# Differential attention of a hybrid decoder step: q and k rows loaded two heads ahead, head 0 prepared amid the projections, and VectorE's small factor and the norm's row written in another form

## The chip, the cores and the metric

One core of a Trainium2 chip runs the whole program in one launch. TensorE multiplies matrices into PSUM, VectorE and ScalarE work element by element on SBUF and PSUM, POOL (GpSimd) does element work and issues DMAs of its own, and SP issues most DMAs. The metric is the time of one execution on the device in microseconds (us). The kernel before takes 2875.54 us, the median of 3 runs (2874.0 to 2877.55).

## The reference

One inference step of a two-layer decoder with fp32 weights: 1024 prompt rows and 16 meta rows (T = 1024, NM = 16), and 8 running sequences of one token each. Layer 0 mixes by gated linear attention, layer 1 by differential attention; each is followed by a squared-ReLU MLP. The change lies in layer 1's prompt part:

```python
def diff_core(q, k, v, q_pos, k_pos, lam):
    s = jnp.einsum('bqhmd,bkhmd->bhmqk', q, k).astype(F32) * (DIFF_DH ** -0.5)
    s = jnp.where(mask, s, -jnp.inf)
    p = jax.nn.softmax(s, axis=-1)
    a = p[:, :, 0] - lam * p[:, :, 1]
    return jnp.einsum('bhqk,bkhe->bqhe', a, v.astype(F32))
...
o = rms_norm(o, g_sub) * (1.0 - lam_init)
```

There are 8 heads, each with two maps m of width 64 over the same values of width 128.

## The kernel before

fp32 products are made from pairs: an operand x is split into a rounded high part and a low part (`split`: ScalarE casts, VectorE subtracts), and three matmuls, high x high, high x low and low x high, are added in PSUM (`mm3`, L187 to L189). All instructions are put in order, engine by engine, by a scheduler that goes by a simulated timeline; on the chip each engine runs its list in order and waits on semaphores. So a source edit can move instructions of other lines.

**Projections** (L1050 to L1089). `XH`, `XL` hold the normalised activations, feature by token, as two halves of 512 tokens. Twelve units u of 256 output columns (u 0 to 3 q, 4 to 7 k, 8 to 11 v) are computed in four blocks of 256 rows (`t2_`). `kunit` loads a unit's weights into the buffers `whi` and `wlo` (two of each). A block's result goes to the buffer `qo` (three of them), is rotated by VectorE if it is q or k, and is written by SP to DRAM (L1078): q to `qd`, k and v to the outputs. The running sequences' decode (`paged`: 512 page loads by SP, element work by VectorE, and small matmuls) is spread over these blocks and most of layer 0.

**Attention** (L1092 on). For each head `prep(h)` loads k and q rows into a `wlo` buffer, the meta keys and the v rows into a `whi` buffer, transposes them on TensorE into the PSUM tile `axt` (L1135, L1140, L1145: 17 transposes) and splits them into the half h % 2 of `XH` and `XL`, which the projections no longer need. For heads 1 to 7, nine DMAs on POOL's queue (`move`, L1151 to L1157) then stack the high and low parts of a map's 64 features in 128 partitions, so that two matmuls do the work of three. Head 0 has no moves: its scores are three matmuls over 64 partitions (L1175 to L1177), those of the others two over 128 (L1179, L1180). `prep(h + 1)` is called ahead of head h's first tile.

`tile_` does one block t of 128 queries: score chunks into `mmt` (three PSUM buffers), VectorE's masked negation with running minimum (L1183, into `as`), ScalarE's exponential with its sum (L1185), the factor -lam l0 / l1 (L1187, L1188), the combination of the two maps (L1189), transposes (L1198), copies (L1200) and the product with v (L1203) into `smt`. After four tiles ScalarE copies the outputs to `Y` (L1238) and the sums of squares are taken (L1239, L1240). After every second head `o_norm` makes the norm's factor, with a power on POOL (L1214), and multiplies the outputs (L1215), on POOL for heads 0 to 6. The buffers of the attention's pools (`as` among them) take memory that the projections' pools (`qo` among them) leave.

Of the kernel before, what the change touches and what calls it, by code (L numbers as in the profile page):

```python
# [21 lines left out]
P = 128  # L22
# [89 lines left out]
def hybrid_step(ctx, tc, A, dbg=None, upto=9):  # L112
# [73 lines left out]
    def mm3(ps, ah, al, bh, bl, first, last):  # L186
        TE.matmul(ps, ah, bh, start=first, stop=False)  # L187
        TE.matmul(ps, ah, bl, start=False, stop=False)  # L188
        TE.matmul(ps, al, bh, start=False, stop=last)  # L189
# [860 lines left out]
    for u in range(12):  # L1050
        hi, lo = kunit(wd, u * 256)
        hv, lv = (x.rearrange("p (k n) -> p k n", n=256) for x in (hi, lo))
        for t2_ in range(4):
            ps = mmt()
            for i in range(2):
                t = 2 * t2_ + i
                a = slice(t * P, (t + 1) * P)
                for k in range(NB):
                    mm3(ps[:, i * 256 : (i + 1) * 256], XH[:, k, a], XL[:, k, a], hv[:, k, :], lv[:, k, :], k == 0, k == NB - 1)
            o = qt.tile([P, 2, 256], F32, name="qo")  # L1060
            S.copy(o.rearrange("p i n -> p (i n)"), ps)
            rows = slice(2 * t2_ * P, (2 * t2_ + 2) * P)
            pr = slice(NM + rows.start, NM + rows.stop)
            if u < 8:
                tmp = qt.tile([P, 2, 4, 16], F32, name="qr")
                pv = ps.rearrange("p (i n d) -> p i n d", i=2, d=64)
                ov = o.rearrange("p i (n d) -> p i n d", d=64)
                tb = rtab[:, 2 * t2_ : 2 * t2_ + 2]
                V.tensor_tensor(ov[:, :, :, 0:16], pv[:, :, :, 0:16], bc(tb[:, :, 0:16], [P, 2, 4, 16], 2), op=ALU.mult)
                V.tensor_tensor(tmp[:, :, :, 0:8], pv[:, :, :, 8:16], bc(tb[:, :, 16:24], [P, 2, 4, 8], 2), op=ALU.mult)  # L1070
                V.tensor_tensor(tmp[:, :, :, 8:16], pv[:, :, :, 0:8], bc(tb[:, :, 24:32], [P, 2, 4, 8], 2), op=ALU.mult)
                steps_v.append(V.tensor_tensor(ov[:, :, :, 0:16], ov[:, :, :, 0:16], tmp, op=ALU.add).ins)
            if u < 4:
                dst = qd[rows, u * 256 : (u + 1) * 256]
            else:
                hs = slice(2 * (u % 4), 2 * (u % 4) + 2)
                dst = A["k_rows_p" if u < 8 else "v_rows_p"][0, 0, pr, hs, :].rearrange("t h d -> t (h d)")
            dma(dst.rearrange("(i p) n -> p i n", p=P), o)  # L1078
            next(paged, None)
        if u == 3:  # L1080
            with tc.issue_after(steps_v[-1]):
                list(alpha_row(A["ln_mlp_g"][0:1], ALU.mult))
        elif u == 6:
# [4 lines left out]
        elif u == 3:  # L1088
            list(paged)  # L1089
# [23 lines left out]
    def prep(h):  # L1113
        kr = A["k_rows_p"][0, 0, :, h, :]
        vr = A["v_rows_p"][0, 0, :, h, :]


        raw = wsp.tile([P, 2048], F32R, name="wlo").bitcast(F32).rearrange("p (i t d) -> p i t d", i=2, d=P)
        kx, qx = raw[:, 0], raw[:, 1]
        vk = wsp.tile([P, 2048], F32R, name="whi").bitcast(F32)  # L1120
        vx = vk[:, :1024].rearrange("p (t d) -> p t d", d=P)
        km, vm = vk[:NM, 1024 : 1024 + P], vms[h % 2]
        dma(kx, kr[NM:].rearrange("(t p) d -> p t d", p=P))
        dma(qx, qd[:, h * P : (h + 1) * P].rearrange("(t p) d -> p t d", p=P))
        dma(km, kr[:NM])
        dma(vm[:NM], vr[:NM])
        dma(vx, vr[NM:].rearrange("(t p) d -> p t d", p=P))
        xh, xl = (x.t[h % 2].rearrange("p a n -> p (a n)") for x in (XH, XL))
        w = NM + T
        k2 = [xh[:, :w], xh[:, w : 2 * w]]  # L1130
        q2 = [xh[:, 2 * w : 2 * w + T], xh[:, 2 * w + T :]]
        kl_, ql2 = xl[:, :w], [xl[:, w : w + T], xl[:, w + T : w + 2 * T]]
        kh_, qh_, ql_ = k2[0], q2[0], ql2[0]
        ps = axt()
        TE.transpose(ps[:, :NM], km, ident[:NM, :NM])  # L1135
        split(kh_[:, :NM], kl_[:, :NM], ps[:, :NM])
        for c in range(2):
            ps = axt()
            for i in range(4):
                TE.transpose(ps[:, i * P : (i + 1) * P], kx[:, 4 * c + i, :], ident)  # L1140
            cs = slice(NM + 512 * c, NM + 512 * c + 512)
            split(kh_[:, cs], kl_[:, cs], ps)
            ps = axt()
            for i in range(4):
                TE.transpose(ps[:, i * P : (i + 1) * P], qx[:, 4 * c + i, :], ident)  # L1145
            cs = slice(512 * c, 512 * c + 512)
            split(qh_[:, cs], ql_[:, cs], ps)
        if h == 0:
            return vm, vx, kh_, qh_, ql_, kl_
        move = nc.gpsimd.dma_start  # L1150
        move(k2[1][64:], kh_[64:])  # L1151
        move(kh_[64:], kl_[:64])
# [415 lines left out]
```

## Time and profile before

| What | us |
|---|---|
| median of 3 runs | 2875.54 |
| the profiled execution | 2875.13 |
| its span | 2873.2 |
| TensorE busy | 2757.3 (96%) |
| VectorE busy | 1974.9 (69%) |
| ScalarE busy | 1083.8 (38%) |
| POOL busy | 1148.1 (40%) |

The span runs from the first to the last instruction. A busy share is an average over stages with different limits, and TensorE's busy time includes the latency of each matmul, so that a busy TensorE is not one at its peak. The views name stretches in us from the span's start; the projections lie at about 1440 to 1775, the attention at 1775 to 2061. In a row of waits stand the waiting engine and line, the releaser, the total, the count and the longest wait.

### The profile page before, as it was taken

The page shows a single profiled execution, that of the slowest core. Times are in us where ns is not written, and L with a number is a line of the kernel's source. Part 1 is how long each engine was busy: PE and PEld are TensorE (multiplying, and loading weights), DVE is VectorE, ACT ScalarE, POOL GpSimd, SP SyncE. Part 2 cuts the span into 40 slices and gives each one's busy share as a digit, 9 for nine tenths or more (in the row PEclk, how much of TensorE's full clock was granted, in tenths as well). Part 3 has the DMA queues.
Part 4 walks back from the last instruction along what each step waited for, and adds up shares of the span by engine and source line. Part 5 has one row for each costly group of instructions (what it writes and reads, how often), then busy time and mean ns, then how long its engine had stood idle before and what let it go on. Part 6 is the DMA issues. An engine that isn't in the chain of part 4 may idle for free. (4 is left out here: it accounts for less than half of the span.)

```text
span 2873.2 us, 52001 instructions
## 1 busy us (share of the span) xinstructions
PE 2757.3 (96%) x19653; PEld 2269.7 (79%) x19653; DVE 1974.9 (69%) x3048; ACT 1083.8 (38%) x2117; POOL 1148.1 (40%) x811
## 2 busy tenths in 40 slices
PE   8889999999999999999999999988999999999997
PEld 5666777997777777777798978878889888797985
DVE  2565544568887778777668711788638888978788
ACT  3233444252221221221331112677525536355553
POOL 1230212334343443433233321032236766777764
PEclk9899999999999999999999998899999999999999
DMA  7557741625798898888569984464334554554573
GB/s 249 180 187 257 250 175 41 245 91 170 282 339 305 319 353 307 322 323 303 198 233 317 363 327 137 89 144 98 118 99 89 114 131 107 136 122 113 128 188 89
DMA packets 276871, 577.28 MB, mean 201 GB/s; under 512 B 24567, under 2 KB 139837, under 8 KB 272525
## 3 DMA queue, kind: packets, MB, share of 16 engines
q1 hardware_dynamic: 252284, 520.66, 51.9%
q0 software_dynamic: 24336, 53.31, 10.7%
q8 instruction: 154, 2.52, 0.4%
q14 instruction: 97, 0.79, 0.1%
HBM read 531.16 MB, written 29.26 MB: 195 GB/s over the span
## 5 line engine op out<-in xcount | busy, mean ns | idle before, releaser
L175 POOL TENSOR_TENSOR wlo<-raw,whi 128x512 fp32r<-128x512 f32 x256 | 372.5, 1469 | 750.5 <-ACT whi L174 669.7
L187 PE MATMUL mmt<-whi,XH 128*128 128x256 f32 (+1 forms) x1760 | 524.5, 300 | 1.1 <-ACT Y L311 0.7
L188 PE MATMUL mmt<-wlo,XH 128*128 128x256 f32 (+1 forms) x1760 | 524.8, 299 | 0.6 <-POOL wlo L175 0.6
L187 PE MATMUL mmt<-XH,whi 128*128 128x512 f32 (+1 forms) x1216 | 436.0, 359 | 7.9 <-DVE HL L184 2.9
L189 PE MATMUL mmt<-whi,XL 128*128 128x256 f32 x1536 | 435.7, 285 | 0.1
L189 PE MATMUL mmt<-XH,wlo 128*128 128x512 f32 (+1 forms) x1216 | 432.2, 356 | 0.0
L174 ACT CAST whi<-raw 128x512 fp32r<-128x512 f32 x256 | 152.6, 619 | 584.1 <-PE mmt L189 181.9
L791 DVE TENSOR_REDUCE sc<-pg 128x16 f32<-128x1024 f32 x256 | 308.3, 1211 | 76.3 <-POOL pg L790 73.8
L188 PEld LDWEIGHTS mmt<-wlo,XH 128*128 128x128 f32 x1760 | 332.1, 189 | 29.0 <-issue 18.1
L187 PEld LDWEIGHTS mmt<-whi,XH 128*128 128x128 f32 x1760 | 331.1, 189 | 25.6 <-issue 11.8
L188 PE MATMUL mmt<-XL,whi 128*128 128x512 f32 x768 | 306.4, 399 | 0.0
L790 DVE TENSOR_TENSOR pg<-pg,qb 128x1024 f32<-128x1024 f32 x192 | 262.3, 1374 | 62.2 <-DMA pg<-in_cache_k 55.4
L189 PEld LDWEIGHTS mmt<-whi,XL 128*128 128x128 f32 x1536 | 289.7, 189 | 11.4 <-issue 10.1
L187 PEld LDWEIGHTS mmt<-XH,whi 128*128 128x128 f32 x1216 | 229.7, 189 | 55.5 <-issue 12.9
L790 POOL TENSOR_TENSOR pg<-pg,qb 128x1024 f32<-128x1024 f32 x64 | 162.3, 2538 | 252.1 <-DMA pg<-in_cache_k 182.6
L189 PEld LDWEIGHTS mmt<-XH,wlo 128*128 128x128 f32 x1216 | 229.8, 189 | 34.5 <-issue 2.1
L187 PE MATMUL mmt<-whi,HH 128*128 128x512 f32 x512 | 204.7, 401 | 4.6 <-DVE Y L1015 4.5
L189 PE MATMUL mmt<-whi,HL 128*128 128x512 f32 x512 | 203.9, 398 | 0.0
L188 PE MATMUL mmt<-wlo,HH 128*128 128x512 f32 x512 | 203.4, 397 | 0.0
L1413 POOL TENSOR_TENSOR wlo<-rw,whi 128x512 fp32r<-128x512 f32 x92 | 157.7, 1779 | 86.2 <-ACT whi L1412 67.7
L1413 POOL TENSOR_TENSOR wlo<-RW,whi 128x512 fp32r<-128x512 f32 x96 | 167.3, 1788 | 53.7 <-ACT whi L1412 53.7
L188 PEld LDWEIGHTS mmt<-XL,whi 128*128 128x128 f32 x768 | 144.9, 189 | 39.1 <-issue 7.9
(440 smaller groups left out, 5837.3 us busy)
## 6 DMA issues: line engine op xcount, KB each, us to landing
pg<-in_cache_k SPq DMA_DIRECT2D x256, 512.0 KB, 6.5
pg<-in_cache_v SPq DMA_DIRECT2D x256, 512.0 KB, 6.4
raw<-in_mlp_w SPq DMA_DIRECT2D x164, 256.0 KB, 4.6
swt<-in_mlp_w SPq DMA_DIRECT2D x32, 1024.0 KB, 5.0
rw<-in_mlp_w SPq DMA_DIRECT2D x116, 256.0 KB, 3.3
RW<-in_mlp_w POOLq DMA_DIRECT2D x96, 256.0 KB, 5.7
raw<-in_gla_w_in SPq DMA_DIRECT2D x48, 256.0 KB, 3.0
swt<-in_gla_w_in SPq DMA_DIRECT2D x12, 1024.0 KB, 4.9
```

Source lines behind the costliest of these rows:

```text
L174: S.copy(hi[:, c], raw)
L175: G.tensor_tensor(lo[:, c], raw, hi[:, c].bitcast(F32), op=ALU.subtract)
L187: TE.matmul(ps, ah, bh, start=first, stop=False)
L188: TE.matmul(ps, ah, bl, start=False, stop=False)
L189: TE.matmul(ps, al, bh, start=False, stop=last)
L790: eng.tensor_tensor(pg, pg, qb, op=ALU.mult)
L791: return V.tensor_reduce(sc[:, n, :], pg.rearrange("p (h d) -> p h d", d=64), op=ALU.add, axis=AX.X).ins
L1413: G.tensor_tensor(lo[:, k, :], t, hi[:, k, :].bitcast(F32), op=ALU.subtract)
```

## The change

q and k rows get buffers of their own (`rqk`, `rkm`, two of each), kept from the projections to the attention's end, and are loaded two heads ahead; the v rows keep their `whi` buffer and are loaded apart. `prep` is cut in two, keys with their three moves first, then queries, and head 0 goes through it as the others do. It is called amid the last blocks of the projections, which are put in an order in which the tokens 0 to 511 are done three blocks before the end. The factor is a scalar_tensor_tensor with one scalar column and a one-column operand. `o_norm` always multiplies on VectorE, in pieces of 512 elements.

```diff
+        return TE.matmul(ps, al, bh, start=False, stop=last)
...
+    rqp = er.enter_context(tc.tile_pool(name="rqp", bufs=2, side="right"))
+    def load_qk(h):
+        raw = rqp.tile([P, 2, 8, P], F32, name="rqk")
+        km = rqp.tile([NM, P], F32, name="rkm")
+        kr = A["k_rows_p"][0, 0, :, h, :]
+        dma(km, kr[:NM])
+        dma(raw[:, 0], kr[NM:].rearrange("(t p) d -> p t d", p=P))
+        dma(raw[:, 1], qd[:, h * P : (h + 1) * P].rearrange("(t p) d -> p t d", p=P))
+        return raw, km
+    def prep(h, raw, km):
...
+        TE.transpose(ps[:, :NM], km, ident[:NM, :NM])
+        split(kh_[:, :NM], kl_[:, :NM], ps[:, :NM])
+        for c in range(2):
+            ps = axt()
+            for i in range(4):
+                TE.transpose(ps[:, i * P : (i + 1) * P], kx[:, 4 * c + i, :], ident)
+            cs = slice(NM + 512 * c, NM + 512 * c + 512)
+            split(kh_[:, cs], kl_[:, cs], ps)
+        move(k2[1][64:], kh_[64:])
+        move(kh_[64:], kl_[:64])
+        move(k2[1][:64], kl_[64:])
+        yield k2, q2, ql2
...
+        for a, b in (q2, ql2):
+            move(b[64:], a[64:])
+            move(b[:64], a[64:])
+            move(a[64:], a[:64])
+        yield
+    blocks = [(u, t) for u in range(10) for t in range(4)]
+    blocks += [(10, 0), (10, 1), (10, 2), (11, 0), (11, 1), (10, 3), (11, 2), (11, 3)]
+    for u, t2_ in blocks:
...
+        if (u, t2_) == (10, 3):
+            nxt = prep(0, *raws[0])
+            with tc.issue_after(outs[-2 * NB]):
+                head = next(nxt)
+                next(nxt)
...
+        elif (u, t2_) == (9, 3):
+            raws = [load_qk(0), load_qk(1)]
...
-                if h == 0:
-                    TE.matmul(ps, q2[r, ts_], k2[r, x:y], start=True, stop=False)
-                    TE.matmul(ps, q2[r, ts_], kl_[r, x:y], start=False, stop=False)
-                    TE.matmul(ps, ql2[r, ts_], k2[r, x:y], start=False, stop=True)
-                else:
-                    TE.matmul(ps, q2[m][:, ts_], k2[m][:, x:y], start=True, stop=False)
-                    TE.matmul(ps, ql2[m][:, ts_], k2[m][:, x:y], start=False, stop=True)
+                TE.matmul(ps, q2[m][:, ts_], k2[m][:, x:y], start=True, stop=False)
+                TE.matmul(ps, ql2[m][:, ts_], k2[m][:, x:y], start=False, stop=True)
...
-        V.tensor_scalar(neg[:, 0:1], neg[:, 1:2], l[:, 0:1], lamv[:, 1:2], ALU.mult, ALU.mult)
+        V.scalar_tensor_tensor(neg[:, 0:1], neg[:, 1:2], lamv[:, 1:2], l[:, 0:1], ALU.mult, ALU.mult)
...
-        eng.tensor_tensor(Yd[:, ts, hs], Yd[:, ts, hs], bc(r, [P, n, m, P], 3), op=ALU.mult)
+        for x in range(0, n, 4 // m if n > 4 else n):
+            a = slice(ts.start + x, ts.start + x + (4 // m if n > 4 else n))
+            V.tensor_tensor(Yd[:, a, hs], Yd[:, a, hs], bc(r[:, a.start - ts.start : a.stop - ts.start], [P, a.stop - a.start, m, P], 3), op=ALU.mult)
...
+            if h < 7:
+                if n == 0:
+                    nxt = prep(h + 1, *raws[h + 1])
+                    hnxt = next(nxt)
+                elif n == 1:
+                    next(nxt)
+                elif n == 3:
+                    vnxt = load_v(h + 1)
+                elif n == 5 and h < 6:
+                    raws.append(load_qk(h + 2))
```

What the scheduler makes of it is shown at three places. In these rows a line number comes first, then the operation, the written and the read tiles and the written shape; `x4` means four in a row.

TensorE at the end of the projections, before (L189 is the last projection matmul, L1135 to L1145 are head 0's transposes, L1175 to L1177 its scores):

```order
L189 MATMUL mmt<-whi,XL_86 128x256
L1135 MATMUL axt<-c_ident,whi 128x16
L1140 MATMUL axt<-c_ident,wlo 128x128 x4
L1145 MATMUL axt<-c_ident,wlo 128x128 x4
L1140 MATMUL axt<-c_ident,wlo 128x128 x4
L1145 MATMUL axt<-c_ident,wlo 128x128 x4
L1175 MATMUL mmt<-XH_83 128x352
L1176 MATMUL mmt<-XL_85,XH_83 128x352
```

and in the changed kernel (L1074 and L1079 are head 1's key transposes, L1191 and L1192 head 0's scores):

```order
L189 MATMUL mmt<-whi,XL_86 128x256
L1074 MATMUL axt<-c_ident,rkm 128x16
L1079 MATMUL axt<-c_ident,rqk 128x128 x8
L1191 MATMUL mmt<-XH_83 128x352 x2
L1192 MATMUL mmt<-XH_83,XL_85 128x352 x2
L1191 MATMUL mmt<-XH_83 128x336
L1192 MATMUL mmt<-XH_83,XL_85 128x336
```

Head 0's own transposes now stand some blocks earlier, nine of head 1's have taken their place, and head 1's other eight come later.

SP's queue at the same place, before (the last `out_v_rows_p<-qo` is the write of the last block; the two loads ahead of it wait for the `wlo` buffer of the last unit):

```order
L1078 DMA out_v_rows_p<-qo 128x2x256 x3
L1123 DMA wlo<-out_k_rows_p 128x8x128
L1124 DMA wlo<-qd 128x8x128
L1078 DMA out_v_rows_p<-qo 128x2x256
L1125 DMA whi<-out_k_rows_p 16x128
L1127 DMA whi<-out_v_rows_p 128x8x128
```

and in the changed kernel:

```order
L1134 DMA out_v_rows_p<-qo 128x2x256 x2
L1175 DMA whi<-out_v_rows_p 128x8x128
L1058 DMA rkm<-out_k_rows_p 16x128
L1134 DMA out_v_rows_p<-qo 128x2x256
L1059 DMA rqk<-out_k_rows_p 128x8x128
L1060 DMA rqk<-qd 128x8x128
```

The last write still stands behind a load that waits for the last unit's buffer (now `whi`), and behind a load of meta keys for head 3, which waits for head 1's first transpose.

POOL's queue around the first power of the norm, before:

```order
L1151 DMA XH_84<-XH_84 64x1040
L1155 DMA XH_84<-XH_84 64x1024
L1156 DMA XH_84<-XH_84 64x1024
L1214 TENSOR_TENSOR orr<-orr,mhalf 128x16
L1153 DMA XH_84<-XL_86 64x1040
L1155 DMA XL_86<-XL_86 64x1024
L1156 DMA XL_86<-XL_86 64x1024
L1152 DMA XH_84<-XL_86 64x1040
L1215 TENSOR_TENSOR Y<-Y,orr 128x8x256
```

and in the changed kernel, POOL and then VectorE (L1225 gives the power its operand, L1229 are the pieces):

```order
L1082 DMA XH_84<-XH_84 64x1040
L1084 DMA XH_84<-XL_86 64x1040
L1083 DMA XH_84<-XL_86 64x1040
L1226 TENSOR_TENSOR orr<-orr,mhalf 128x16
L1093 DMA XH_84<-XH_84 64x1024
```

```order
L1225 SCALAR_TENSOR_TENSOR orr<-oss,orr 128x16
L1200 SCALAR_TENSOR_TENSOR ast<-ast,lamv,ls 128x1
L1195 ISA as,ast<-mmt,cmask 128x464
L1195 ISA ast 128x1
L1201 SCALAR_TENSOR_TENSOR as<-as,ast 128x784
L184 TENSOR_TENSOR XL_86<-axt,XH_84 128x512
L1195 ISA as,ast<-mmt,cmask,ast 128x448
```

Some eight more rows of VectorE follow before the four pieces. The power now stands behind all three key moves, of which L1083 may start only when L1082 has landed, and POOL's multiply is gone. At the second and the third of these places the same three moves stand ahead of the power.

More of the change, by code (lines that the diff above doesn't have):

```diff
@@ L1049, in hybrid_step @@
     qd = A["qd"]
[L1050 to L1074, printed above, removed]
-            else:
[L1076 to L1080, printed above, removed]
@@ L1111, in hybrid_step, with load_v, tile_ @@
         G.memset(x, 0.0)
-    def prep(h):
-        kr = A["k_rows_p"][0, 0, :, h, :]
+    def load_v(h):
         vr = A["v_rows_p"][0, 0, :, h, :]
[L1118 to L1125, printed above, removed]
+        vx = wsp.tile([P, 2048], F32R, name="whi").bitcast(F32)[:, :1024].rearrange("p (t d) -> p t d", d=P)
+        vm = vms[h % 2]
         dma(vm[:NM], vr[:NM])
         dma(vx, vr[NM:].rearrange("(t p) d -> p t d", p=P))
[L1128 to L1147, printed above, removed]
-        if h == 0:
[L1149 to L1152, printed above, removed]
-        move(k2[1][:64], kl_[64:])
-        for a, b in (q2, ql2):
-            move(b[64:], a[64:])
-            move(b[:64], a[64:])
-            move(a[64:], a[:64])
-        return vm, vx, k2, q2, ql2, None
-    def tile_(h, t, out, vm, vx, k2, q2, ql2, kl_):
+        return vm, vx
+    def tile_(h, t, out, vm, vx, k2, q2, ql2):
         W = NM + P * (t + 1)
@@ L1223, in o_fm @@
         V.scalar_tensor_tensor(XL[:, h, cs], ps, gs, XH[:, h, cs].bitcast(F32), ALU.mult, ALU.subtract)
-    nxt = prep(0)
+    vnxt = load_v(0)
     for h in range(8):
-        head = nxt
+        if h:
+            head = hnxt
+        vh = vnxt
         for n, t in enumerate((3, 2, 1, 0, 7, 6, 5, 4) if h == 7 else (7, 1, 5, 3, 6, 0, 4, 2)):
-            if n == 0 and h < 7:
-                nxt = prep(h + 1)
+            if h < 7:
[8 more added lines that the diff above has]
+                    raws.append(load_qk(h + 2))
             if n % 4 == 0:
@@ L1234, in hybrid_step @@
             at = t % 4 if h == 7 else t // 2
-            tile_(h, t, po[:, at * P : (at + 1) * P], *head)
+            tile_(h, t, po[:, at * P : (at + 1) * P], *vh, *head)
             if n % 4 == 3:
```

66 lines of the change are left out of this document (54 added, 12 removed).

## The prediction

> **What bounds the kernel now.** I read the mean of each stretch first, since the page's 96% for TensorE says only that it is never long without work. The windows view (length, then busy time and count of PE, PEld, DVE, ACT and POOL, the granted clock, DMA share, GB/s) for the projections, the attention, its opening, and three later stretches:
>
> ```profile
> 1440.00:1775.00 335.00, 330.72 (x3028) 298.10 (x3026) 172.82 (x266) 69.81 (x125) 98.48 (x67) 0.99 0.79 281
> 1775.00:2061.00 286.00, 256.87 (x1786) 230.72 (x1786) 228.52 (x717) 192.91 (x453) 62.19 (x76) 0.92 0.48 110
> 1775.00:1782.00 7.00, 3.86 (x26) 3.04 (x25) 2.75 (x5) 2.75 (x6) 0.00 (x0) 0.90 0.93 270
> 1782.00:1802.00 20.00, 18.93 (x75) 15.66 (x76) 15.12 (x51) 10.68 (x24) 4.34 (x8) 0.50 0.93 206
> 1802.00:1817.00 15.00, 15.00 (x106) 12.66 (x105) 8.37 (x29) 8.82 (x20) 0.51 (x1) 0.92 0.12 24
> 1840.00:1856.00 16.00, 12.13 (x76) 11.51 (x75) 7.99 (x29) 8.14 (x20) 1.02 (x2) 0.79 0.51 91
> 1872.00:1878.00 6.00, 2.85 (x23) 2.60 (x23) 5.96 (x11) 2.80 (x8) 5.60 (x5) 1.00 1.30 246
> 1990.00:2000.00 10.00, 9.31 (x68) 7.93 (x69) 10.00 (x35) 8.09 (x18) 5.78 (x7) 1.00 0.46 107
> ```
>
> The projections are TensorE at full clock; nothing is to be had there. The attention has a granted clock of 0.92 and two engines that take turns: TensorE busy for 257 of its 286 us, VectorE for 229. The diff touches little else, so its price is read in these 286 us. Its opening is the odd part. The copies that end each head (one of two per head, ScalarE) show it:
>
> ```profile
> 1826.42 0.56 ACT L1238 COPY Y<-smt 128x512 f32<-128x512 f32 x1
> 1861.01 0.56 ACT L1238 COPY Y<-smt 128x512 f32<-128x512 f32 x1
> 2020.13 0.56 ACT L1238 COPY Y<-smt 128x512 f32<-128x512 f32 x1
> ```
>
> Head 0 ends 51.4 us after the projections (1775.0), the heads 1 to 6 take (2020.1 - 1826.4)/6 = 32.3 us each. Why the opening is long: the chain of waits has TensorE's last transposes of head 0, then a load; the timelines of SP and VectorE show a second wait beside it, with the landing times of the projections' output writes and of the v rows (two tile views) below.
>
> ```profile
> 1775.61 0.44 PE axt L1145 x4
> 1776.49 5.60 DMA whi<-out_k_rows_p
> 1782.49 1.05 PE axt L1140 x4
> 1785.27 0.29 PE mmt L1177
> 1775.87 0.53 SPq L1078 DMA_DIRECT2D out_v_rows_p<-qo  x1
> 1777.14 0.42 SPq L1127 DMA_DIRECT2D whi<-out_v_rows_p  x1
> 1782.28 0.52 DVE L1183 CUSTOM_DVE_ANT_0 as<-mmt,cmask 128x352 f32<-128x352 f32 x1 [3.27 <-DMA whi<-out_v_rows_p]
> DMA to landing us min/median/max: 4.5/6.6/7.5
> DMA to landing us min/median/max: 3.8/3.8/3.8
> ```
>
> The view names the v rows as what released VectorE's first score, but those land at 1777.14 + 3.8 = 1780.9. The last write of `qo`, issued at 1775.87, lands by its median at 1782.5, and the score starts at 1782.28: that write is the gate. It makes sense in the program, because the `as` buffers take the memory that the projections' `qo` buffers leave, and may be written only when the last of these is out. So two waits end together at 1782.3: head 1's meta keys for TensorE, and this write for VectorE. Removing the first alone moves no start.
>
> **The change part by part**, against the profiled execution's own 2875.1 us (the median shown is 2875.5, so both are taken as one).
>
> *Head 0 amid the projections.* Two timeline rows, ScalarE's copy of a block's result and VectorE's first split of head 0:
>
> ```profile
> 1769.28 0.59 ACT L1061 COPY qo<-mmt 128x512 f32<-128x512 f32 x1 [5.12 <-PE mmt L189]
> 1775.63 0.17 DVE L184 TENSOR_TENSOR XL<-axt,XH 128x16 fp32r<-128x16 f32 x1 [36.70 <-ACT XH L183]
> ```
>
> 17 transposes go among the projections' last three blocks, which are TensorE-bound. Four cost 0.44 us (L1145 above), so 17 cost **+1.9 us**. Before, they ran while VectorE was shut out until 1782.3 anyway, so what they leave there is idle time. Their splits (VectorE was idle for 36.7 us) and nine moves (POOL, idle too) are hidden by those blocks, 3 x 5.7 = 17 us; without that cover the moves, of which some wait for others to land, would hold the first scores back by two landings of 5.6 us (median of the moves, below).
>
> *Head 0 itself.* The gate stays: in the new order the last `qo` write still stands behind a load that waits for TensorE's end, as before. The first score therefore still starts about 7.5 us after the projections' end, and the clock will still fall, since TensorE finds even less to do until then. From there the gain is work that is no longer in the half-clock stretch, where TensorE is busy 18.93 of 20 us: the third score matmul (L1177, 28 of them; 14 stand in that stretch at 0.29 us, 4.1 us; the other 14 cost about half, some 2 us) and nine of head 1's 17 transposes, now run before the gate opens (9 x 1.05/4 = 2.4 us). Together 8.5 us of TensorE, but VectorE is busy 15.12 of those 20 us, and only 1.5 us of that (three splits) moves out. So the stretch cannot fall by more than 20 - 13.6 = 6.4 us; the next one, with VectorE at 8.37 of 15, can give its 2. Bounds -4.1 (the matmuls of the stretch alone) to -8.5, taken **-6.5 us**, nearer to VectorE's limit.
>
> *Loads two heads ahead.* TensorE's waits for them and for the moves behind them, head 2's load in the chain, and head 0's third score matmuls:
>
> ```profile
> PE axt L1135 <- DMA whi<-out_k_rows_p: 4.3, 4, 2.2
> PE mmt L1179 <- DMA XH<-XH: 2.7, 1, 2.7
> PE mmt L1180 <- DMA XL<-XL: 1.2, 1, 1.2
> 1826.27 1.52 DMA whi<-out_k_rows_p
> L1177 PE MATMUL mmt<-XH,XL x28: 272/412/585, 1779.4 to 1815.9; 64*128 64x352 f32 x4, 64*128 64x336 f32 x4, 64*128 64x272 f32 x4, 64*128 64x400 f32 x4
> ```
>
> Of the first, 2.2 us is the opening, 2.1 us lies in three later heads, where the load waits for a `whi` buffer that the head before still reads: **-1 us**, half of it, since VectorE has work to catch up on (bounds 0 to -2.1). For heads 0 and 1 the loads now stand in SP's queue amid the projections, and two of them wait there for rows just written to land (6.6 us by the median above), with the decode's pages and a unit's weights queued behind. The weights come a unit of 4 x 5.7 = 23 us ahead, so I take 0; without that lead TensorE would wait up to 6 us each time. The other two are the start of head 2, 3.9 us of TensorE idle, and then a clock of 0.79 over 1840 to 1856, up to 16 x 0.21 = 3.4 us. Head 2's load is issued at 1826.27 before; its operands' room is free when head 0's last score is done, 1815.9. Now the keys lie ready by then and are moved first, so their moves can start up to 10 us earlier. VectorE is busy for only 8 of those 16 us, so most comes through: **-4.5 us** (0, if the moves are late again, to -7.3).
>
> *The norm's row.* Groups by shape, two instances, and the splits of the same size as the new pieces:
>
> ```profile
> L1189 DVE SCALAR_TENSOR_TENSOR as<-as,ast 128x528 f32<-128x528 f32 x8 | 18.3, 2290 | 0.1
> L1215 POOL TENSOR_TENSOR Y<-Y,orr 128x2048 f32<-128x2048 f32 x3 | 11.0, 3655 | 0.0
> 1872.89 4.72 DVE L1189 SCALAR_TENSOR_TENSOR as<-as,ast 128x528 f32<-128x528 f32 x1
> 1873.39 3.65 POOL L1215 TENSOR_TENSOR Y<-Y,orr 128x2048 f32<-128x2048 f32 x1
> 2021.02 0.77 DVE L1189 SCALAR_TENSOR_TENSOR as<-as,ast 128x528 f32<-128x528 f32 x1
> 1868.10 1.28 DVE L184 TENSOR_TENSOR XL<-axt,XH 128x512 fp32r<-128x512 f32 x2
> ```
>
> The same instruction takes 0.77 us alone and 4.72 us beside POOL's multiply: VectorE stands still for as long as POOL reads. Three such places cost 18.3 - 8 x 0.77 = 12.1 us of VectorE, and TensorE is busy for only 2.85 of the 6 us there. The 12 pieces of 512 replace it at about 0.6 us (two splits in a row take 1.28), 7.5 us; head 6's two pieces against POOL's 1024 elements cancel. Net -4.6. POOL's power stays ahead of the pieces, and they stand some ten VectorE instructions behind its operands, so it matters whether it is late (the power; the landing of the moves that start a head's set, and of all moves within XH):
>
> ```profile
> 1868.42 2.93 POOL L1214 TENSOR_TENSOR orr<-orr,mhalf 128x16 f32<-128x16 f32 x1
> XH<-XH POOLq DMA_DIRECT2D x7, 260.0 KB, 3.1
> DMA to landing us min/median/max: 2.8/5.6/9.9
> ```
>
> In all three places POOL's queue now holds, ahead of the power, a move that waits for another to land: 0.5 + 3.1 + 0.5 + 2.9 = 7.0 us from the last key split, against about 7 us of VectorE work before the pieces. Just in time. With the longest landing, 9.9 us, it is 6.8 us late, three times, and VectorE with every later score waits behind the first piece: 20.4 - 4.6 = +16. Taken **-4.5 us**, by the 3.1 of that very move (+16 to -12.1, if the pieces fall into VectorE's idle time).
>
> *The maps' factor.*
>
> ```profile
> L1188 DVE TENSOR_SCALAR ast<-ast,ls,lamv 128x1 f32<-128x1 f32 x64 | 17.2, 270 | 0.7
> L1187 DVE RECIPROCAL ast<-ls 128x1 f32<-128x1 f32 x64 | 10.0, 158 | 4.2 <-ACT as L1185 3.5
> L1223 DVE SCALAR_TENSOR_TENSOR XL<-axt,gs,XH 128x512 fp32r<-128x512 f32 x16 | 11.7, 734 | 6.5 <-ACT XH L1222 6.4
> L184 DVE TENSOR_TENSOR XL<-axt,XH 128x512 fp32r<-128x512 f32 x32 | 21.4, 683 | 0.6 <-ACT XH L183 0.6
> ```
>
> A one-column instruction with no scalar column costs 158 ns, with two 270; one scalar column adds 734 - 683 = 51 ns at 512 elements. The new form, one scalar column and a one-column second operand, is not in the trace: between 158 and 270, taken 210. 64 x 60 ns = 3.8 us of VectorE, of which about half lies where VectorE is the limit: **-2 us** (0 to -7).
>
> Sum: +1.9 - 6.5 - 1 - 4.5 - 4.5 - 2 = -16.6, so **2858.5 us**. All good ends together give -35, all bad ones +1.9 - 4.1 + 16 = +14.
>
> **The rivals.**
>
> *The gains do not add (chance 0.20).* VectorE at 229 of 286 us becomes the bound: TensorE's savings in heads 0 and 2 shrink to 2 and 0 us, the rest stands: +1.9 - 2 - 0.5 - 4.5 - 2 = -7, 2868 us. For it: in the first part of a head VectorE has no idle time left (1990 to 2000). Against it: in 1802 to 1817 and 1840 to 1856 it is half idle.
>
> *The clock recovers early (0.13).* If the half clock ended soon after the gate opened, as it does in a few us after 1850, head 0 would run at VectorE's pace and the clock's dips at later heads would go too: 6 us more in head 0, 4 us in the others, 2848 us. Against it: 20 us at 0.50 though TensorE was busy for 18.93. [...]
>
> *The half clock stays (0.18; the slower side).* [...] Each us at 0.50 costs 0.5 us where TensorE is the limit. From 45 us beyond the 20 of before, that is until about 1850, the whole gain of 16.6 and 5.8 more are lost; through head 1's end (59 us more) it is 13 us slower, 2888 us. For it: the 20 us just named. Against it: it came back at 1802 to 1817 with the same kind of work.
>
> *It doesn't do what it says (0.05).* The scheduler's order moves the waits, not ends them: 2874 us.
>
> **How the numbers follow.** The forecast has 0.44: 2858.5, own range 2850 to 2867. 0.2% is 5.8 us, about what a measurement can tell from no change. Faster by more: the forecast, the early clock, and three quarters of the first rival, 0.44 + 0.13 + 0.15 = 0.72. Same: 0.05 + 0.05 = 0.10. Slower: 0.18. The range, 2843 to 2878, holds the first two rivals, no change, and a half clock that lasts up to 39 us longer (2858.5 + 19.5); it leaves out the rest of the slower case, and the ends of the bounds, which would have to fall together.
>
> **What would show it.** Right: projections that end near 1777; the first score still about 7.5 us later; head 0 ending 5 to 8 us closer to them; no TensorE wait for moves at head 2; no 4 to 5 us instance of the 528-element combine; a factor near 210 ns. Wrong: a first score that starts within 3 us of the projections' end (then the gate was misread and the gain is larger), VectorE idle before the pieces for POOL, a clock of 0.5 past head 0, or TensorE idle in the projections behind SP's new loads.

## The result, and the profile after

| | before | changed |
|---|---|---|
| median (14 runs each) | 2877.48 us | 2879.69 us |
| ratio, with 95% interval | | 1.0005 (0.9995 to 1.0016) |
| profiled execution, its span | 2873.2 us | 2873.4 us |

The change made no difference that can be measured. 2858.5 us had been forecast, so 16.6 us of expected gain are missing. The stages of the two profiled executions, taken from ScalarE's copies (the first and last projection result, the second copy of `Y` of a head):

| Stage | before, us | changed, us | difference |
|---|---|---|---|
| up to the first projection result | 1452.0 | 1453.4 | +1.3 |
| projections, first to last result | 322.9 | 328.2 | +5.3 |
| head 0, from the last projection result | 51.5 | 48.5 | -3.0 |
| heads 1 to 6 | 193.7 | 195.7 | +2.0 |
| head 7 | 40.5 | 40.6 | +0.1 |
| the rest | 812.6 | 807.1 | -5.4 |

The rest holds no edit. Over the profiles of this study it takes 801.4 to 812.6 us, so its 5.4 us are not counted as an effect of the change. A few us in any one stage are not an effect by themselves either: run 2 below leaves the attention's instructions on TensorE, VectorE, ScalarE and POOL in the order of the changed kernel, and its profile has 289.7 us there against 284.8.

The rows of ScalarE's timeline behind the table, for the changed kernel (start, duration, engine, line):

```profile
1781.51 0.59 ACT L1117 COPY qo<-mmt 128x512 f32<-128x512 f32 x1 [5.12 <-PE mmt L189]
1829.97 0.59 ACT L1262 COPY Y<-smt 128x512 f32<-128x512 f32 x1 [1.13 <-PE smt L1215]
2025.66 0.57 ACT L1262 COPY Y<-smt 128x512 f32<-128x512 f32 x1
```

The same stretches by engine, first of the kernel before (head 0), then of the changed one (the projections' stretch in which TensorE idles, head 0, its opening, the start of head 2); the columns are those of the windows view above:

```profile
1775.40:1827.00 51.60, 47.11 (x275) 40.14 (x273) 35.14 (x117) 29.82 (x70) 4.85 (x9) 0.77 0.52 123
```

```profile
1700.00:1720.00 20.00, 16.86 (x150) 12.07 (x149) 0.33 (x1) 0.93 (x2) 2.83 (x5) 0.91 0.89 331
1781.50:1830.60 49.10, 38.63 (x239) 35.10 (x239) 32.33 (x114) 27.37 (x66) 5.09 (x10) 0.83 0.46 107
1782.00:1802.00 20.00, 12.98 (x62) 10.48 (x61) 11.95 (x44) 8.48 (x21) 1.78 (x4) 0.74 0.49 120
1840.00:1856.00 16.00, 9.83 (x55) 8.68 (x54) 7.64 (x33) 8.32 (x22) 1.02 (x2) 0.82 0.69 135
```

TensorE is busy for 47.11 - 38.63 = 8.5 us less in head 0, which is what was expected, and the clock is better: 0.74 over the 20 us behind the projections' end, where the kernel before has 0.90 for 7 us and then 0.50 for 20. But head 0 is only 2.5 us shorter between these marks: TensorE now stands idle for 10.5 of 49.1 us. VectorE's 12 us in the opening's 20 show that it is not the limit there either. Something else ends last. TensorE's timeline and waits name it:

```profile
1785.00 0.56 PE L1191 MATMUL mmt<-XH 128*128 128x352 f32 x2 [2.38 <-DMA XH<-XH]
1788.00 0.95 PE L1192 MATMUL mmt<-XH,XL 128*128 128x352 f32 x2 [2.44 <-DMA XL<-XL]
1815.88 0.40 PE L1191 MATMUL mmt<-XH 128*128 128x352 f32 x1 [2.75 <-issue]
1850.86 0.63 PE L1191 MATMUL mmt<-XH 128*128 128x352 f32 x1 [5.47 <-issue]
1852.13 0.66 PE L1192 MATMUL mmt<-XH,XL 128*128 128x352 f32 x1 [0.65 <-DMA XL<-XL]
1916.29 0.75 PE L1191 MATMUL mmt<-XH 128*128 128x352 f32 x3 [2.63 <-DMA XH<-XH]
2014.28 0.39 PE L1192 MATMUL mmt<-XH,XL 128*128 128x272 f32 x1 [0.53 <-DMA XL<-XL]
```

These are first scores of heads 0, 1, 2, 4 and 7, waiting for the moves that stack their operands. ("issue" is a wait for which the view has no releaser; both rows stand at a head's first score, right behind a landing move.) At the starts of heads 1 to 7 these waits sum to 16.2 us. In the kernel before, only head 2 has such a wait, 2.7 + 1.2 us. How near each head's start is to its moves is read from POOL's and TensorE's rows: the time from the issue of the last move to the head's first score that reads it (352 wide, in head 7 272 wide).

| us from last move to score | head 1 | 2 | 3 | 4 | 5 | 6 | 7 |
|---|---|---|---|---|---|---|---|
| before | 14.9 | **2.9** | 7.8 | 5.2 | 7.8 | 4.4 | 7.5 |
| changed | **2.9** | **3.3** | **2.9** | **2.9** | **2.9** | **2.9** | **3.0** |

The landing itself takes 2.8 to 3.2 us in these heads of the changed kernel; a head with such a number starts when its last move lands. Before, one head did. Now all seven do.

### The profile page after: what moved, and what is told of

It reads as the page before. It is cut to its first block, busy times and chain, and to the rows that moved or that the text cites. A ratio compares the mean times of both kernels' runs of the same rounds, so it can differ in the third digit from the quotient of the medians.

```text
span 2873.4 us, 51968 instructions
## 1 busy us (share of the span) xinstructions
PE 2749.2 (96%) x19625; PEld 2275.5 (79%) x19625; DVE 1955.4 (68%) x3062; ACT 1084.5 (38%) x2117; POOL 1146.9 (40%) x816
## 5 line engine op out<-in xcount | busy, mean ns | idle before, releaser
L189 PE MATMUL mmt<-whi,XL 128*128 128x256 f32 x1536 | 436.5, 286 | 0.0
L189 PE MATMUL mmt<-XH,wlo 128*128 128x512 f32 (+1 forms) x1216 | 432.3, 356 | 0.0
L189 PEld LDWEIGHTS mmt<-whi,XL 128*128 128x128 f32 x1536 | 291.7, 190 | 8.8 <-issue 8.0
L189 PEld LDWEIGHTS mmt<-XH,wlo 128*128 128x128 f32 x1216 | 230.1, 189 | 34.5 <-issue 2.1
L189 PE MATMUL mmt<-whi,HL 128*128 128x512 f32 x512 | 204.6, 400 | 0.0
L1438 POOL TENSOR_TENSOR wlo<-RW,whi 128x512 fp32r<-128x512 f32 x96 | 169.4, 1795 | 50.8 <-ACT whi L1437 50.6
```

The lines of the kernel that those rows point to most:

```text
L189: return TE.matmul(ps, al, bh, start=False, stop=last)
L1438: G.tensor_tensor(lo[:, k, :], t, hi[:, k, :].bitcast(F32), op=ALU.subtract)
```

## The experiments

All runs of a kernel (6 or 12) are compared with runs of the kernel before on the same chip (17 or 23); a ratio is to that kernel's time, and its interval covers 95%. The stages of a run are read from one profiled execution each.

**1. Preparation sooner.** Before the change a head's keys and queries are transposed within a few us: 6 to 10 matmuls lie between the last key transpose and the last query transpose of the heads 1 to 7. Cut in two, the queries come late, by 43 to 69 matmuls: TensorE's rows for head 2 in the changed kernel (L1079 keys, L1089 queries), and POOL's moves behind them (start, duration to issue, idle time before).

```profile
1827.37 0.60 PE L1079 MATMUL axt<-c_ident,rqk 128*128 128x128 f32 x4
1829.77 0.60 PE L1079 MATMUL axt<-c_ident,rqk 128*128 128x128 f32 x4
1833.42 0.60 PE L1089 MATMUL axt<-c_ident,rqk 128*128 128x128 f32 x4
1834.98 0.60 PE L1089 MATMUL axt<-c_ident,rqk 128*128 128x128 f32 x4
```

```profile
1831.34 0.51 POOL L1082 DMA_DIRECT2D XH<-XH  x1 [16.01 <-ACT XH L183]
1835.98 0.51 POOL L1083 DMA_DIRECT2D XH<-XL  x1 [2.64 <-DMA XH<-XH]
1837.25 0.51 POOL L1093 DMA_DIRECT2D XH<-XH  x1 [0.76 <-ACT XH L183]
1847.92 0.51 POOL L1095 DMA_DIRECT2D XH<-XH  x1 [8.50 <-DMA XH<-XH]
1848.87 0.51 POOL L1095 DMA_DIRECT2D XL<-XL  x1 [0.44 <-DMA XL<-XL]
```

The chain runs from 1831.34 to 1848.87, 17.5 us (15.9 before), and begins no sooner than before (1831.01), although SP issued the load of these rows at 1767.34, 59 us ahead of their first transpose: what holds it is where the scheduler put the transposes, not the load. The edit calls the whole preparation of head h + 1 right behind the scores of the last tile of head h - 1, and the loads, still two heads ahead, at a head's first tile:

```diff
     def tile_(h, t, out, vm, vx, k2, q2, ql2, mid=None):
...
+        if mid:
+            mid()
         for m in range(2):
             S.activation(sc_[:, m, :W], ...)
...
-                if n == 0:
-                    nxt = prep(h + 1, *raws[h + 1])
-                    hnxt = next(nxt)
-                elif n == 1:
-                    next(nxt)
+                if n == 0:
+                    if h == 0:
+                        pre(1)
+                    hnxt = ahead
+                    if h < 6:
+                        raws.append(load_qk(h + 2))
...
-            tile_(h, t, po[...], *vh, *head)
+            tile_(h, t, po[...], *vh, *head, mid=(lambda: pre(h + 2)) if n == 7 and h < 6 else None)
```

> The changed kernel with head h+1's keys and queries prepared together, right behind the scores of the last tile of head h-1 (instead of keys ahead of the first tile of head h and queries a tile later), and the loads two heads ahead at a head's first tile. Theory A, the moves are late: in the changed kernel TensorE waits 16.2 us at the heads' starts for the last moves (3.9 us before the change), since a head's queries are transposed 40 to 66 matmuls behind its keys; here they stand 15 to 35 behind. The waits for moves fall to 5 us or less, the attention gets 8 to 12 us shorter (from 285 to about 275), the time falls to about 2869. Rival B, VectorE and the clock set the attention's length: the waits move elsewhere, the attention stays within 3 us of 285. Rival C, what comes after the attention absorbs it: the attention gets shorter, the span does not.

Measured: 2858.46 us, ratio 0.9935 (0.9919 to 0.9951); attention 269.8 us (284.8 in the changed kernel). The same rows:

```profile
1822.26 0.60 PE L1079 MATMUL axt<-c_ident,rqk 128*128 128x128 f32 x4
1823.58 0.60 PE L1089 MATMUL axt<-c_ident,rqk 128*128 128x128 f32 x4
1839.42 0.51 POOL L1095 DMA_DIRECT2D XL<-XL  x1 [2.64 <-DMA XL<-XL]
1847.69 0.32 PE L1192 MATMUL mmt<-XH,XL 128*128 128x352 f32 x1
```

Head 2's score now comes 8.3 us behind its last move, and the row of the table above reads 10.4, 8.3, 3.9, 2.9, 7.3, 9.0, 2.9. The waits at the starts of heads 1 to 7 fall from 16.2 to 2.7 us; another 5.9 us are head 0's. Theory A holds, with twice the price expected: 0.7% or 20 us against the change. Rival C falls: what comes after the attention took 809 us, 2 more than in the changed kernel. The edit does two things at once, it joins the two halves (14 to 16 matmuls from the last key to the last query) and it calls them sooner; no run separates them.

**2. The memsets off POOL's queue.** In the changed kernel the projections lose time at one place. POOL's timeline and TensorE's row behind it:

```profile
1695.08 1.29 POOL L175 TENSOR_TENSOR wlo<-raw,whi 128x512 fp32r<-128x512 f32 x1 [9.00 <-ACT whi L174]
1705.75 0.34 POOL L1167 MEMSET vm<- 128x128 f32 x2 [9.38 <-SPq L757]
1706.06 1.26 POOL L175 TENSOR_TENSOR wlo<-raw,whi 128x512 fp32r<-128x512 f32 x1
```

```profile
1707.38 0.58 PE L188 MATMUL mmt<-wlo,XH 128*128 128x256 f32 x1 [3.14 <-POOL wlo L175]
```

The memsets of `vm` wait for the decode's page buffers. A weight split that the next unit needs has slipped behind them; in the kernel before, this split stands ahead of them, and TensorE does not wait. The diff never touched that line; it is the scheduler's new order.

```diff
     for x in vms:
-        G.memset(x, 0.0)
+        V.memset(x, 0.0)
```

> The changed kernel with the two memsets of vm on VectorE instead of POOL; no other instruction moves. In the changed kernel the last weight split of unit 9 stands on POOL behind these memsets, which wait for the decode's pages until 1705.75, and TensorE waits 3.1 us for it. Theory A: that wait and the clock of 0.91 that follows it (1.8 us) are gone; the projections end 4 to 5 us earlier, the time falls by 4 to 5 us. Rival: the weights themselves come late by SP's queue (its loads stand behind those of the q and k rows), so the wait stays: 0 us. Rival C, later stages absorb it: projections end earlier, time within 1 us of the changed kernel.

Measured: 2871.60 us, 0.9986 (0.9971 to 1.0001), some 0.2% or 5.5 us under the change. TensorE's wait for that split is gone (0.4 us for an earlier one stays), and the projections take 319.2 us. Of these 9.0 us less, 4.6 lie between the 33rd and the 37th of the 48 results, where the memsets stood; the rest lies ahead of them, where the order of the two kernels is the same, so it is a difference between two executions. As expected by theory A, at the edge of what the interval tells apart.

**3. The last write off the gate.** `qo` and `qr` get buffers that no tile of the attention uses.

```diff
-    qt = e.enter_context(tc.tile_pool(name="qt", bufs=3))
...
     er = ExitStack()
+    qt = er.enter_context(tc.tile_pool(name="qt", bufs=3, side="right"))
```

> The changed kernel with the buffers of qo and qr in memory of their own, so that no score waits for the last qo write. Theory of the prediction (that write is the gate): VectorE's first score starts when TensorE has one, that is when head 0's last query moves land, about 2 us sooner after the projections' end than in the changed kernel (8.5 us becomes 6.5), and 2 us are gained in head 0, no more. Rival: the write was not the gate; the first score stays 8.5 us behind the projections' end. Rival: the moves of head 0 also land sooner and the first score comes within 4 us: 4 us or more gained.

Measured: 2880.29 us, 1.0010 (0.9997 to 1.0023). VectorE's first score came 8.2 us behind the last projection result instead of 8.4. In the changed kernel that write does release it; with the write out of the way the next thing does (VectorE's timeline, changed kernel and then this run):

```profile
1789.94 0.52 DVE L1195 CUSTOM_DVE_ANT_0 as<-mmt,cmask 128x352 f32<-128x352 f32 x1 [5.81 <-DMA out_v_rows_p<-qo]
```

```profile
1794.23 0.52 DVE L1195 CUSTOM_DVE_ANT_0 as<-mmt,cmask 128x352 f32<-128x352 f32 x1 [6.17 <-PE mmt L1192]
```

So the write was one of two gates that open within 2 us of each other; the other is head 0's last query move, behind which TensorE's score starts at 1788.00 in the changed kernel. The expected 6.5 us did not come about, in part because that move landed 7.4 us behind the projections' end in this run, and not 6.5. A run without a gain told which of the two had to go next.

**4. All three.** The edits of 1, 2 and 3 together.

> The three edits of the other runs together: preparation sooner, memsets on VectorE, qo's buffers off the gate. Theory A: they add up, 8 to 12 plus 4 to 5 plus 2 us, so 2861 to 2866 us, ratio to the kernel before about 0.995. Rival C: what comes after the attention gives back a third or more of it: 2868 or more. Rival B: within 5 us of the changed kernel but for the 4 to 5 us of the memsets.

Measured: 2851.52 us, 0.9916 (0.9902 to 0.9930). They add up: 0.70% of run 1, 0.19% of run 2 and nothing of run 3 make 0.89%, and 0.89% under the change is what is measured. That it fits to the last digit is luck, since each of these has an interval of about 0.2%.

**5. Head 0 a block sooner.** On top of run 4:

```diff
-    blocks += [(10, 0), (10, 1), (10, 2), (11, 0), (11, 1), (10, 3), (11, 2), (11, 3)]
+    blocks += [(10, 0), (10, 1), (11, 0), (11, 1), (10, 2), (10, 3), (11, 2), (11, 3)]
...
-        if (u, t2_) == (10, 3):
+        if (u, t2_) == (10, 2):
```

> The fourth run (all three edits) with head 0's preparation one projection block (5.7 us) sooner: the tokens 0 to 511 are done four blocks before the end. Theory A for the opening: the first score now waits for head 0's last query moves (they land about 7.5 us behind the projections' end, TensorE waits 2.8 and 2.4 us for them); with 5.7 us more the waits vanish, the first score comes 2 to 3 us behind the projections' end (8.1 in the fourth run), head 0 takes 4 to 5 us less than its 44.0, the time falls to about 2847. Rival: the moves land as late relative to the end (their landing is set by the loads and writes that share the DMA engines there): first score still more than 6 us behind, 0 us. Rival: the weights of unit 11 are not there one block earlier, TensorE waits in the projections: 0 or slower.

Measured: 2846.70 us, 0.9885 (0.9861 to 0.9909), the best of the study: 32 us under the kernel before, and 0.3% under run 4, which is just what the intervals can tell apart. The last projection result, VectorE's first score and the opening's window:

```profile
1780.38 0.59 ACT L1117 COPY qo<-mmt 128x512 f32<-128x512 f32 x1 [5.07 <-PE mmt L189]
1782.31 0.51 DVE L1195 CUSTOM_DVE_ANT_0 as<-mmt,cmask 128x352 f32<-128x352 f32 x1
1817.04 0.57 ACT L1270 COPY Y<-smt 128x512 f32<-128x512 f32 x1
```

```profile
1780.00:1800.00 20.00, 17.67 (x112) 15.58 (x111) 17.43 (x63) 14.48 (x32) 4.47 (x9) 0.91 1.00 199
```

1.9 us from the projections' end to the first score, a clock of 0.91 over the 20 us behind it (before: 0.90 for 7 us, then 0.50 for 20), and 36.7 us for head 0 (44.0 in run 4, 51.5 before). TensorE no longer waits for head 0's moves. With both gates open, head 0 gets shorter by more than the 6.5 us that were forecast with the gate in its place.

**6 to 8, and 11 and 12: the norm's row and the factor.** Run 6 is run 1 with both as before the change; run 7 the kernel before with both new; 8, 11 and 12 are the changed kernel with both old, the norm old, the factor old. The edits are the diff's own lines, turned back or (7) applied alone; the norm turned back reads

```diff
-        for x in range(0, n, 4 // m if n > 4 else n):
-            a = slice(...)
-            V.tensor_tensor(Yd[:, a, hs], ...)
+        (G if n > 4 else V).tensor_tensor(Yd[:, ts, hs], Yd[:, ts, hs], bc(r, [P, n, m, P], 3), op=ALU.mult)
```

> The first run (preparation sooner) with the norm's multiplication on POOL and the factor's tensor_scalar as before the change. By the prediction's terms the norm is worth 4.5 us and the factor 2: 6.5 us slower than the first run, about 2865. Rival, VectorE has room once the moves are on time: within 2 us of the first run. Rival: VectorE is the limit now, so that the whole lock (12 us) and factor (3.6 us) count: 12 us or more slower.

> The kernel before with the norm's row and the factor of the change, nothing else. By the prediction's terms 6.5 us faster than before, about 2870. Rival: both are hidden, or the power stands behind POOL's moves and VectorE waits for it: within 2 us of before. If what comes after the attention takes 807 us as in the changed kernel (812.6 before), the gain there comes from these two edits.

> The changed kernel with the norm and the factor as before: only loads and preparation are changed. By the prediction's terms 6.5 us slower than the changed kernel, about 2885, with the same late moves (10 us or more of waits for them). Rival, the moves bind and hide what VectorE does: within 2 us of the changed kernel. If what comes after the attention takes about 807 us, that gain comes from the loads' part (the output weights' loads stand elsewhere); if 812, from norm or factor.

> The changed kernel with only the norm's multiplication back on POOL; the new factor stays. If the norm is what made the run with old norm and factor 0.3% faster than the change: about 2869, ratio 0.997. If it was the factor: about 2878, like the change. By the prediction's term: 4.5 us slower than the change.

> The changed kernel with only the factor back as a tensor_scalar; the norm in pieces stays. The run with both back was 0.5% faster than the one with only the norm back. If the factor's form itself (or the order that comes with it) costs that: about 2866, ratio 0.996 or less. If the two runs differ by chance of their orders (the queries' transposes stand up to 71 matmuls behind the keys' in the one, up to 70 in the other): here, with 48 to 66, within 4 us of the changed kernel. By the prediction's term: 2 us slower than the change.

| Run | ratio to before | interval |
|---|---|---|
| 6, sooner, both old (run 1, both new: 0.9935) | 0.9919 | 0.9898 to 0.9939 |
| 7, before, both new | 1.0012 | 0.9995 to 1.0029 |
| 8, changed, both old | 0.9973 | 0.9957 to 0.9988 |
| 11, changed, norm old | 1.0027 | 1.0011 to 1.0043 |
| 12, changed, factor old | 1.0000 | 0.9983 to 1.0016 |
| the change, both new | 1.0005 | 0.9995 to 1.0016 |

Run 7 is the plain one: VectorE is relieved, the 528-element combine takes 764 ns in the mean and the factor 217, and nothing is gained. The times from last move to first score suggest why: 2.9, 3.6, 2.9, 2.9, 3.5 and 2.9 us for heads 2 to 7. VectorE got to the heads' ends sooner, and met the moves there. Run 6 shows that this is not all: with the preparation sooner, norm and factor as before are 0.16% faster than the new ones, where the prediction's terms ask for 0.23% slower, which the intervals leave out. POOL's multiplication costs little in that run: it holds one combine for 1.1 us, where the kernel before lost 12.1 us (the rows are in the last section).

The change and the runs 8, 11 and 12 do not make a sum. With the new factor, the new norm is 0.22% faster than the old one (1.0005 to 1.0027); with the old factor it is 0.27% slower (1.0000 to 0.9973). Both differences are just beyond what the intervals tell apart. Run 8 fits neither of the times expected for it, run 11 is slower as the prediction's term says, and run 12 cannot be told from the change. Each of these edits gives TensorE another order (in run 11 the last query transpose of the heads 4 to 6 stands 63 to 67 matmuls behind the last key transpose, in run 12 43 to 45), so the order is the likely cause, but no run holds it fixed, and why run 8 came out best of these four stays open. The length of the chains of moves does not explain it: summed over heads 3 to 7, from first to last move, it is 91.5 us in run 8, 104.4 in run 11, 86.2 in the changed kernel and 81.4 in run 12.

**9. The last moves twice, in the kernel before.** If the chain of moves already set the pace before, lengthening it must cost its full length.

```diff
             move(a[64:], a[:64])
+            move(a[64:], a[:64])
```

> The kernel before with the last two moves of each head (the one onto the upper half of the queries, high and low) done twice, the second behind the landing of the first; values are the same. Loop theory: the stretch from the last score of head h-1 to the first score of head h+1 (transposes, splits, nine moves, their landings; 32 us) already set the heads' pace in the kernel before, though only 3.9 us of it show as waits. Then a chain that is longer by one landing (4 to 6 us) makes each of the heads 1 to 7 longer by about as much: attention 20 to 35 us longer, about 2900 to 2910 us. Theory of the prediction (TensorE and VectorE take turns, the moves are covered except at head 2): 4 to 8 us slower at most.

Measured: 2885.17 us, 1.0029 (1.0012 to 1.0047): 8.5 us slower. The chains of heads 1 to 7 got longer by 1.3 to 4.2 us, less than expected, 20.6 us in sum; the loop theory would have all of it in the time, and falls in the form stated. Before the change the heads 3 to 6 had 1.5 to 4.9 us to spare above the 2.9 (the table), and this absorbs most of a landing. The moves did not set the pace before; they stood a few us behind what did.

**10. The best with POOL's norm.** Run 5 with the norm's old line.

> The fifth run with the norm's multiplication on POOL as before the change, the new factor kept. If the row in pieces costs more than it saves, as the pair of the runs with old norm and factor suggests (0.2 to 0.3% to the old ones' favour), 2 to 8 us faster than the fifth run, ratio to before 0.986 or less. By the prediction's term 4.5 us slower, 0.990.

Measured: 2847.75 us, 0.9899 (0.9872 to 0.9927), 0.14% above run 5. The intervals reach nearly 0.4% either way, so this run tells neither no difference nor the 4.5 us apart. Its moves are not all on time either: at the heads' starts it waits 10.6 us for them, run 5 only 2.1.

## Why the prediction was wrong

The change was forecast to gain 16.6 us and gained none; what it lacked was moves in time. Run 1, which brings them, is at the time forecast (2858.46 against 2858.5), but that is luck: run 6 gets there without the terms for norm and factor. By the prediction's own steps:

- **Loads two heads ahead (-4.5, and -1): the step that failed.** "Now the keys lie ready by then and are moved first, so their moves can start up to 10 us earlier." The first move of head 2 was issued at 1831.34, before at 1831.01. A load that comes early moves nothing when the transposes behind it stand in a list whose order is fixed; the prediction read the order at the projections' end and at the norm, not the distance from a head's keys to its queries (43 to 69 matmuls, 6 to 10 before). And the last move of a set counts, not the first. The price was the opposite of the forecast: waits for moves at the starts of all seven heads, 16.2 us where 3.9 had been, and run 1 gives 20 us back.
- **Head 0 (-6.5).** TensorE's busy time fell by the 8.5 us computed, though in part by the better clock (0.83 for 0.77 over head 0): the transposes of the scores and the products with v, which no edit touches, take 20.4 us and not 21.6. The stretch did not follow (-3.0). The gate was read rightly, by the write that releases it and by its 7.5 us (8.4 measured), but the sentence that the moves are hidden by three blocks, 17 us, was wrong: from the first issue (1764.47) to the last landing they take 23.5 us, and land at 1788, 6.5 us after the last block. Run 5, with the other edits too, shows the size of what was there, 14.8 us.
- **Head 0 amid the projections (+1.9).** The stage grew by 5.3 us. The transposes fit: the block that holds them takes 7.8 us and not 5.7, 2.1 us more. The rest is no more than the 3.1 us of wait that run 2 removes with the 1.8 us of lower clock behind it (0.91 over 1700 to 1720). The bound of "up to 6 us" was put on SP's loads; it came by POOL's queue.
- **Norm (-4.5).** Mechanism right, gain absent. The 4.7 us instances are gone (the group below), the pieces take 684 ns at the median and not 0.6 us (a split in the prediction's own rows takes 683), and VectorE waits 3.2 us for the power in three places, as feared but short. In run 7 none of it reached the time, where the moves end last; that it stays out in run 6 as well shows that the moves are not the whole reason.
- **Factor (-2).** The instruction takes 214 ns; 210 was taken. Its gain was as absent, in the same runs.
- **The rivals.** The one given 0.05, that the scheduler's order moves the waits and does not end them, comes nearest in mechanism and in time (2874 us). "The gains do not add" named VectorE as the bound, with 12 of 20 us busy in the opening. The half clock did not stay (0.74, then 0.97 by 1802 to 1817), and the early clock, which did come in head 0 (1.00 over 1796 to 1802, before 0.50), bought nothing while TensorE had nothing to do; over the whole attention the granted clock is 0.92 as before. No rival named the moves' chain, though the prediction's own bound did ("if the moves are late again") and its rows showed it (3.9 us at head 2).

The groups of the changed kernel that belong to the last points (group, duration of all and mean ns of one, idle time before):

```profile
L1201 DVE SCALAR_TENSOR_TENSOR as<-as,ast 128x528 f32<-128x528 f32 x8 | 6.1, 763 | 0.0
L1200 DVE SCALAR_TENSOR_TENSOR ast<-ast,lamv,ls 128x1 f32<-128x1 f32 x64 | 13.7, 214 | 0.4
```

## What to carry to other kernels

Where two engines seem to take turns, list for every turn the slack of each thing that must have arrived, not only the waits: a chain with 2 us to spare shows no wait, and takes over as soon as the engines get faster or the chain a little later. When operands are loaded sooner, follow them to the last step ahead of their use, and check in the order of each engine that those steps moved too. A change worth a few us of one engine is not measured by itself where a scheduler rewrites the order around it, so compare the orders of the two kernels before a small difference is put down to the edit.

## What the runs showed of the hardware

POOL's multiplication did not stop VectorE as such. In run 6 a score beside it, which reads `mmt` in PSUM and the mask, kept its time (0.56 us, and 0.57 us just ahead of it; 566 ns is the mean in the changed kernel); so did the old factor (0.27 us; 270 ns in the mean before), which reads one tensor in SBUF and two scalar columns. A combine, which reads two tensors in SBUF, took 2.27 us for 912 elements (1159 ns is its mean in the changed kernel, where VectorE multiplies the outputs). VectorE's and POOL's rows in run 6:

```profile
1932.01 0.57 DVE L1195 CUSTOM_DVE_ANT_0 as<-mmt,cmask 128x400 f32<-128x400 f32 x1
1932.59 3.62 POOL L1229 TENSOR_TENSOR Y<-Y,orr 128x2048 f32<-128x2048 f32 x1
1933.10 0.56 DVE L1195 CUSTOM_DVE_ANT_0 as<-mmt,cmask 128x400 f32<-128x400 f32 x1
...
1867.42 3.62 POOL L1229 TENSOR_TENSOR Y<-Y,orr 128x2048 f32<-128x2048 f32 x1
1869.44 0.27 DVE L1202 TENSOR_SCALAR ast<-ast,ls,lamv 128x1 f32<-128x1 f32 x1
1869.75 2.27 DVE L1203 SCALAR_TENSOR_TENSOR as<-as,ast 128x912 f32<-128x912 f32 x1
```

The new factor has a second tensor operand, and beside POOL's multiplication in run 10 one column took 3.86 us (214 ns is its mean in the changed kernel):

```profile
1922.64 3.86 DVE L1202 SCALAR_TENSOR_TENSOR ast<-ast,lamv,ls 128x1 f32<-128x1 f32 x1
1922.86 3.62 POOL L1229 TENSOR_TENSOR Y<-Y,orr 128x2048 f32<-128x2048 f32 x1
```

So the 12.1 us of the kernel before came from the neighbour that the order happened to give POOL's instruction: three combines of 528 elements took 4.72, 5.03 and 4.74 us beside it, and 0.77 us elsewhere.

The granted clock, by the windows of the kernel before: 0.50 over 1782 to 1802, where TensorE was busy for 18.93 of the 20 us and 42 of its 75 matmuls were scores over 64 partitions. From 1800.39 to 1805.62 all matmuls were over 128 partitions; the clock was 0.50 until 1804, 0.89 over the next 2 us, and 1.00 over 1806 to 1808.

```profile
1800.00:1802.00 2.00, 2.00 (x9) 1.61 (x8) 1.62 (x7) 0.83 (x2) 0.00 (x0) 0.50 1.25 223
1802.00:1804.00 2.00, 2.00 (x12) 2.00 (x11) 0.70 (x1) 0.48 (x1) 0.51 (x1) 0.50 0.45 82
1804.00:1806.00 2.00, 2.00 (x17) 1.82 (x17) 0.00 (x0) 0.60 (x2) 0.00 (x0) 0.89 0.45 90
```

It was 0.50 over 1850 to 1854 as well, where all matmuls were over 128 partitions and TensorE was busy throughout, and 1.00 over 1856 to 1860. In the changed kernel, where all scores use 128 partitions, it was 0.50 over 1788 to 1795, 0.66 over 1795 to 1796 and 1.00 over 1796 to 1798, with TensorE busy for 12.98 of the 20 us from 1782. So the width of the scores alone does not tell the clock; what sets it, no run tried.
